# The FFN output product with activations as the stationary operand, and its last three units bank by bank

## The chip, the cores and the metric

The kernel runs on one core of a Trainium2 chip. The metric is the device time of one execution in microseconds (us), as the median of several runs. One execution is also profiled; the profile's times are counted from the first instruction of the program.

## What is computed

Two transformer-like blocks over 256 tokens (T) of width 1024 (D), in float32. The change lies in the end of the second block:

```python
h = modulate(rmsnorm_2(x, norm_ffn_g[l]), sh_f, sc_f)
a, b = jnp.split(h @ w_ffn_in[l], 2, axis=-1)
x = x + g_f[:, None, :] * ((jax.nn.silu(a) * b) @ w_ffn_out[l])
...
return rmsnorm_2(x, norm_final_g)
```

w_ffn_in is 1024 x 5632, w_ffn_out 2816 x 1024. g_f has one value for each of the 1024 features. The final norm divides each token's row by its root mean square over the 1024 features and multiplies by norm_final_g.

## The kernel before

x is kept with features on partitions: 8 chunks of 128 features, each 128 x 256 tokens. Every product is made of three matmuls (`mm3`, lines 156 to 161): each float32 operand is split into a rounded part and the rest (hi and lo), and hi*hi, lo*hi and hi*lo are summed in PSUM. The first operand of a matmul is the stationary one, which is loaded into the array; the second is moved through it.

Weights come in units of 128 x 1024. `unit_order` (line 1453) lists them in the order of use. SyncE loads two units at a time (line 92), ScalarE or VectorE rounds one to hi (lines 106 and 108), VectorE subtracts to get lo (line 116). `fill` (line 97) keeps this some five units ahead of the use, and is called whenever a unit is taken (`w`, line 120).

The order of instructions on each engine is the order of the program text; each engine takes its own instructions strictly in that order. A DMA is issued by the engine on whose queue the text puts it, and its wait stands in that engine's order.

The FFN is the last part of `block2`, from line 1365 on. It first makes the norm's row factor and the modulated input (`h`, lines 1368 and 1369), then the scaled gate `hgf` (line 1371, 128 x 8, feature within its chunk on partitions), then finishes two pairs of w_ffn_in units whose products were made ahead (lines 1381 to 1388). The loop over the 22 pairs (line 1390) makes, for each j, two products of w_ffn_in (16 x 3 matmuls of 256 columns in all, PSUM tiles from `main`), Tanh on ScalarE (line 1400), two VectorE steps (1401, 1407) and the split into fh and fl (1408, 1409): 128 hidden features x 256 tokens. From j = 3 on it takes unit j-3 of w_ffn_out in `kunit` (line 242): for each of the 8 chunks of output features the weights are stationary (128 x 128) and fh or fl is moved (256 columns), and the sums stay in four PSUM banks over all 22 units, two feature chunks to a bank.

After the loop come the last three units (lines 1419 to 1422). Then, for each chunk, VectorE adds the gated product to x (1428), and TensorE transposes the result to token rows (1431, two 128 x 128 transposes a chunk) into four PSUM tiles. ScalarE squares and sums each (1436), VectorE multiplies each by the final gain `fg` (1438, 1442), and after Ln, Exp (lines 257, 258) and a refining step on VectorE (264 to 266) the rows are scaled (1447, 1449) and written out by four DMAs of 256 KB on SyncE's queue (1450).

Of the kernel before, what the change touches and what calls it, by code (L numbers as in the profile page):

```python
# [13 lines left out]
F32 = mybir.dt.float32  # L14
# [5 lines left out]
AF = mybir.ActivationFunctionType  # L20
OP = mybir.AluOpType
AX = mybir.AxisListType
PSUM = bass.MemoryType.PSUM
DRAM = bass.MemoryType.DRAM

T = 256
D = 1024
# [37 lines left out]
class Kx:  # L65
# [1008 lines left out]
    def block2(self):  # L1074
        nc, tc, a = self.nc, self.tc, self.a
        mt = self.mod[1]
        x = self.x
        with ExitStack() as ctx:
            big = ctx.enter_context(tc.tile_pool(name="b2", bufs=1))
            tmp = ctx.enter_context(tc.tile_pool(name="b2t", bufs=2))  # L1080
            self.side_cycle = ("s",)
            fg = self.sm("final_g")
# [75 lines left out]
            z = big.tile([128, 4, PAD + T], F32, name="z")  # L1158
# [57 lines left out]
            for c in range(4):  # L1216
# [7 lines left out]
                else:  # L1224
                    if c == 2:
                        p, pz = self.units("w_u", 4, h, lambda i: self.bank(2 + i), False)
                        self.fill()
                    else:
                        p = self.unit("w_u", 2 * c, h)
# [13 lines left out]
            p = self.unit("w_qi", 4, h)  # L1243
# [5 lines left out]
            for u in range(4):  # L1249
                p = self.unit("w_qi", u, h)  # L1250
# [59 lines left out]
            for u in range(8):  # L1310
                p = self.unit("w_qk", u, h)
# [11 lines left out]
            for u in range(16):  # L1323
                p = self.unit("w_g", u, h)
# [7 lines left out]
            for n in range(8):  # L1332
                if n % 2 == 0:
                    w = self.w("w_conv_proj", n // 2)
                p = self.main()[:, :T]
# [8 lines left out]
            banks = [self.bank(i) for i in range(4)]  # L1344
            for n in range(9):
                if n < 8:
                    if n % 2 == 0:
                        w = self.w("w_attn_proj", n // 2)
                    p = self.main()[:, :T]
                    self.chunk(w, (ah, al), p, nk=4, off=(n % 2) * 512)  # L1350
                    t = gates[:, n]
# [13 lines left out]
        with ExitStack() as ctx:  # L1365
            big = ctx.enter_context(tc.tile_pool(name="f2", bufs=1))
            tmp = ctx.enter_context(tc.tile_pool(name="f2t", bufs=5))
            rstd = self.row_rstd(self.ps_x[:, :T], "exp_and_others")
            h = self.modulated(rstd, gn, mt[:, 24:32])
            hgf = big.tile([128, 8], F32, name="hgf")  # L1370
            nc.scalar.mul(hgf, mt[:, 40:48], 0.5)
            nf = a["w_ffn_out"].shape[0]
            fg = big.tile([128, 2, 512], F32, name="fg")
            act = {}

            def ffn_out(j):
                self.kunit("w_ffn_out", j, act.pop(j), banks, j == 0, j == nf - 1)

            raw = [[tmp.tile([128, T], F32, name=f"st{k}", bufs=2) for k in range(3)] for _ in range(2)]
            bias = []  # L1380
            for j in range(2):
                t, b = self.settle_raw(2 * j, rstd, raw[j][0])
                bias.append((b, self.settle_raw(2 * j + 1, rstd, raw[j][1])[1]))
                self.fill(self.pos + 4 + j, self.pos + 4 + j)
                half = self.normp.tile([128, 1], F32, name="stb", bufs=6)
                nc.vector.tensor_scalar(half, b, 0.5, None, op0=OP.mult)
                nc.scalar.activation(raw[j][2], t, AF.Tanh, bias=half, scale=0.5)
                nc.scalar.activation(t, t, AF.Identity, bias=b)
            self.fill(self.pos + 6, self.pos + 6)
            for j in range(nf):  # L1390
                sa = tmp.tile([128, T], F32, name="sa")
                if j < 2:
                    p, q, th = raw[j]
                else:
                    if j == 2:
                        p, q = self.units("w_ffn_in", 4, h, lambda i: self.side(), False)
                    else:
                        p = self.unit("w_ffn_in", 2 * j, h)
                    th = sa
                    nc.scalar.activation(th, p, AF.Tanh, scale=0.5)  # L1400
                nc.vector.scalar_tensor_tensor(sa, th, 1.0, p, op0=OP.add, op1=OP.mult)
                if j > 2:
                    q = self.unit("w_ffn_in", 2 * j + 1, h)
                if j < 2:
                    nc.vector.scalar_tensor_tensor(sa, q, bias[j][1], sa, op0=OP.add, op1=OP.mult)
                else:
                    nc.vector.tensor_tensor(sa, q, sa, op=OP.mult)
                act[j] = tuple(tmp.tile([128, T], F32R, name=n) for n in ("fh", "fl"))
                self.split(*act[j], sa)
                if j == 3:  # L1410
                    banks = [self.bank(i) for i in range(4)]
                if j == 2:
                    self.fill()
                if j == 10:
                    nc.sync.dma_start(fg, bass.AP(tensor=a["gf"].tensor, offset=a["gf"].offset,
                                                  ap=[[0, 128], [512, 2], [1, 512]]))
                if j >= 3:
                    ffn_out(j - 3)
            for j in range(nf - 3, nf - 1):
                ffn_out(j)  # L1420
            self.lnexp()
            ffn_out(nf - 1)
            tok = [[self.main(), self.main()], [self.side(), self.side()]]
            z = big.tile([128, 2, 2, 512], F32, name="z")
            ss = [big.tile([128, 2], F32, name=f"ss{i}") for i in range(2)]
            for n in range(8):
                xc = x[:, n]
                nc.vector.scalar_tensor_tensor(xc, banks[n // 2][:, (n % 2) * T:(n % 2 + 1) * T], hgf[:, n:n + 1], xc,
                                               op0=OP.mult, op1=OP.add)
                for tt in range(2):  # L1430
                    nc.tensor.transpose(tok[tt][n // 4][:, (n % 4) * 128:(n % 4 + 1) * 128],
                                        xc[:, tt * 128:(tt + 1) * 128], self.ident)
            for i in range(2):
                for tt in range(2):
                    junk = tmp.tile([128, 512], F32, name="junk", bufs=2)
                    nc.scalar.activation(junk, tok[tt][i], AF.Square, scale=1.0 / 32, accum_out=ss[i][:, tt:tt + 1])
            for tt, i in ((0, 0), (1, 0), (0, 1)):
                nc.vector.tensor_tensor(z[:, tt, i], tok[tt][i], fg[:, i], op=OP.mult)
            ms = tmp.tile([128, 2], F32, name="ms")
            nc.vector.tensor_tensor(ms, ss[0], ss[1], op=OP.add)  # L1440
            rs = self.rsqrt_start(ms, [128, 2], tmp)
            nc.vector.tensor_tensor(z[:, 1, 1], tok[1][1], fg[:, 1], op=OP.mult)
            rstd = self.rsqrt_end(rs)
            for tt, i in ((0, 0), (1, 1), (1, 0), (0, 1)):
                y = z[:, tt, i]
                if tt == i == 1:
                    nc.scalar.mul(y, y, rstd[:, tt:tt + 1])
                else:
                    nc.vector.tensor_scalar(y, y, rstd[:, tt:tt + 1], None, op0=OP.mult)
                nc.sync.dma_start(self.out[tt][:, i * 512:(i + 1) * 512], y)  # L1450


def unit_order():
# [145 lines left out]
```

## Time and profile before

| | us |
|---|---|
| median of 3 runs | 1450.75 (1449.32 to 1452.83) |
| the profiled execution | 1445.74 |
| its span, first to last instruction | 1443.7 |
| TensorE busy | 1367.2 (95%) |
| VectorE busy | 1098.1 (76%) |
| ScalarE busy | 770.9 (53%) |
| FFN, from the gate to the end | about 190 |

TensorE's busy time is that of pipelined matmuls: a matmul of 256 columns is shown with 0.28 us, but the next one starts 0.12 us after it. What counts for the pace is the distance between starts. The chain that ended last is put down to TensorE for 71%, to VectorE for 21%, to ScalarE for 3% and to DMA for 3%. In the text PE is TensorE, PEld its loading of stationary operands, DVE is VectorE, ACT ScalarE, SP SyncE.

### The profile page before, as it was taken

To read this page: it belongs to the slowest core of one execution; us is meant where nothing else is said; L and a number is where in the kernel's file an instruction comes from. 1 tells how busy PE (TensorE), PEld (TensorE's weight loads), DVE (VectorE), ACT (ScalarE), POOL (GpSimd) and SP (SyncE) were. 2 spreads that over 40 slices of the span, in tenths; PEclk is the share of its full clock that TensorE was granted. 3 is DMA by queue.
4 is the path that set the end of the run, shared out by engine and by line. 5 is a ranking of instruction groups with operands and counts; after the bars stand their busy time and mean duration, and the time that the engine had idled before them with its cause. 6 is when DMAs were issued, how large, how long until landed. Compare 5 with 4: busy or idle time off the path is not lost.

```text
span 1443.7 us, 27450 instructions
## 1 busy us (share of the span) xinstructions
PE 1367.2 (95%) x11208; PEld 1321.7 (92%) x11208; DVE 1098.1 (76%) x2105; ACT 770.9 (53%) x1247; POOL 115.4 (8%) x93
## 2 busy tenths in 40 slices
PE   3888999989999999999999999999999899999997
PEld 2767889979999999999999999999999889999997
DVE  7887899996999487777777766666799968765554
ACT  3535665444999545454444454444565484644442
POOL 0020010000000000000000000000167620100000
PEclk8999999999999999999999999999999999999999
DMA  9566554544777888888888867766445335345551
GB/s 376 182 210 216 207 178 147 177 145 146 263 275 280 321 307 291 297 305 315 306 295 283 287 228 240 235 218 219 144 163 175 117 109 208 123 175 190 180 196 64
DMA packets 106062, 317.31 MB, mean 220 GB/s; under 512 B 5584, under 2 KB 34640, under 8 KB 103632
## 3 DMA queue, kind: packets, MB, share of 16 engines
q1 hardware_dynamic: 65696, 250.54, 49.5%
q10 hardware_dynamic: 39408, 61.87, 12.2%
q0 software_dynamic: 832, 3.15, 0.7%
q8 instruction: 88, 1.44, 0.4%
q14 instruction: 38, 0.31, 0.1%
HBM read 297.71 MB, written 17.83 MB: 219 GB/s over the span
## 4 chain that ended last, share of the span: by engine, by line
PE 71%; DVE 21%; ACT 3%; DMA 3%; issue 2%; POOL 0%; POOLq 0%; DVEq 0%; SPq 0%; ACTq 0%
PE m L159 12%; PE m L160 12%; PE m L161 12%; PE a L160 11%; PE a L161 10%; PE a L159 10%; DVE wlo L116 5%; DVE a L1168 3%; DVE junk L322 2%; PE s L983 2%; DMA raw<-in_ada_w 1%; DMA mraw<-in_ada_w 1%; DVE score L1127 1%; DVE cacc L552 1%; ACT whi L108 1%
## 5 line engine op out<-in xcount | busy, mean ns | idle before, releaser
L159 PE MATMUL m<-hi,whi 128*128 128x256 f32 x1816 | 519.3, 286 | 7.1 <-DVE cacc L552 4.0
L161 PE MATMUL m<-hi,wlo 128*128 128x256 f32 x1816 | 509.8, 281 | 2.8 <-POOL wlo L116 1.5
L160 PE MATMUL m<-lo,whi 128*128 128x256 f32 x1816 | 509.6, 281 | 0.0
L116 DVE TENSOR_TENSOR wlo<-raw,whi 128x1024 fp32r<-128x1024 f32 x398 | 479.0, 1222 | 36.3 <-ACT whi L108 25.8
L108 ACT CAST whi<-raw 128x1024 fp32r<-128x1024 f32 x428 | 444.4, 1045 | 50.9 <-DMA raw<-in_peer_v 17.9
L159 PEld LDWEIGHTS m<-hi,whi 128*128 128x128 f32 x1816 | 343.7, 189 | 10.0 <-issue 4.2
L161 PEld LDWEIGHTS m<-hi,wlo 128*128 128x128 f32 x1816 | 343.3, 189 | 3.4 <-DVE wlo L116 1.7
L160 PEld LDWEIGHTS m<-lo,whi 128*128 128x128 f32 x1816 | 343.3, 189 | 0.6
L161 PE MATMUL a<-wh,wlo 128*128 128x256 f32 x1024 | 288.3, 282 | 0.0
L160 PE MATMUL a<-wl,whi 128*128 128x256 f32 x1024 | 288.2, 281 | 0.0
L159 PE MATMUL a<-wh,whi 128*128 128x256 f32 x1024 | 287.9, 281 | 0.0
L161 PEld LDWEIGHTS a<-wh,wlo 128*128 128x128 f32 x1024 | 192.9, 188 | 0.0
L160 PEld LDWEIGHTS a<-wl,whi 128*128 128x128 f32 x1024 | 192.7, 188 | 0.0
L159 PEld LDWEIGHTS a<-wh,whi 128*128 128x128 f32 x1024 | 192.6, 188 | 0.0
L1024 DVE TENSOR_TENSOR wl<-act,wh 128x256 fp32r<-128x256 f32 x128 | 54.5, 425 | 140.5 <-PE a L160 125.2
L790 ACT ACTIVATE act<-m 128x256 f32<-128x256 f32 x126 | 48.4, 384 | 167.2 <-PE m L161 167.2
L1019 ACT CAST wh<-act 128x256 fp32r<-128x256 f32 x128 | 51.9, 406 | 145.4 <-DVE act L1012 121.5
L322 DVE SCALAR_TENSOR_TENSOR junk<-mraw,silu 128x1024 bf16<-128x1024 f32 x80 | 97.5, 1219 | 7.5 <-DMA mraw<-in_ada_w 6.9
L116 POOL TENSOR_TENSOR wlo<-raw,whi 128x1024 fp32r<-128x1024 f32 x33 | 79.2, 2425 | 36.0 <-ACT whi L108 26.5
L986 ACT ACTIVATE stg<-s 128x512 f32<-128x512 f32 x64 | 64.2, 1108 | 3.1 <-PE s L983 1.0
L1012 DVE TENSOR_TENSOR act<-act,gt 128x256 f32<-128x256 f32 x128 | 53.6, 419 | 8.2 <-DMA gt<-gd 8.2
L159 PE MATMUL a<-fh,whi 128*128 128x256 f32 x176 | 50.6, 287 | 3.4 <-ACT fh L250 3.4
(443 smaller groups left out, 1772.8 us busy)
## 6 DMA issues: line engine op xcount, KB each, us to landing
raw<-in_peer_u SPq DMA_DIRECT2D x64, 1024.0 KB, 6.0
raw<-in_peer_v SPq DMA_DIRECT2D x64, 1024.0 KB, 5.1
mraw<-in_w_ada ACTq DMA_DIRECT2D x48, 512.0 KB, 5.5
raw<-in_w_ffn_in SPq DMA_DIRECT2D x22, 1024.0 KB, 5.1
gd<-stg ACTq DMA_DIRECT2D x16, 1024.0 KB, 6.2
gt<-gd ACTq DMA_DIRECT2D x14, 1024.0 KB, 7.5
mraw<-in_ada_w SPq DMA_DIRECT2D x24, 512.0 KB, 4.4
raw<-in_w_ffn_out SPq DMA_DIRECT2D x11, 1024.0 KB, 4.9
```

Of the source, the lines that this page charges most:

```text
L108: self.nc.scalar.copy(t, self.raw[k])
L116: eng.tensor_tensor(t, self.raw.pop(k), h.bitcast(F32), op=OP.subtract)
L159: mm(out, w[0], x[0], start=start, stop=False, **kw)
L160: mm(out, w[0], x[1], start=False, stop=False, **kw)
L161: mm(out, w[1], x[0], start=False, stop=stop, **kw)
L322: self.nc.vector.scalar_tensor_tensor(junk, w, 0.5, self.silu_c[i], op0=OP.mult, op1=OP.mult, accum_out=self.mod[i][:, u:u + 1])
L790: nc.scalar.activation(t, p, AF.Gelu)
L986: nc.scalar.mul(stg[:, :, e0:e0 + 4].rearrange("p i t -> p t i"), p, 1.0 / GSCALE)
L1012: nc.vector.tensor_tensor(tv, tv, gv, op=OP.mult)
L1019: nc.scalar.copy(wts[b], acts[b])
L1024: nc.vector.tensor_tensor(wl, acts.pop(b), wts[b].bitcast(F32), op=OP.subtract)
L1168: nc.vector.scalar_tensor_tensor(zp, z[:, c, k:k + T], w, zp, op0=OP.mult, op1=OP.add)
```

## The change

- The product with w_ffn_out is made the other way round: fh and fl, 128 tokens at a time, are stationary, and 512 columns of the weights are moved. A unit is 2 token halves x 2 column halves x 3 matmuls of 512 columns. Each of the four banks now holds one token half and one half of the output features, in token rows.
- The gate must then be a row that is the same on all partitions. It is written to a DRAM tile `grow` with features in order, and read back into all 128 partitions (`gb`), both by DMAs on ScalarE's queue, right after line 1371.
- x is transposed to token rows (`xt`) during the loop, in four groups of four transposes after j = 5, 7, 9 and 11, each group copied out of PSUM by ScalarE.
- The last three units run bank by bank: for each of the four banks the nine matmuls of all three units, and then that bank's gate, residual, square and final gain; after both banks of a token half its norm and output.

```diff
             def ffn_out(j):
-                self.kunit("w_ffn_out", j, act.pop(j), banks, j == 0, j == nf - 1)
+            def ffn_out(j, w, tt, i):
+                s, m = slice(tt * 128, (tt + 1) * 128), slice(i * 512, (i + 1) * 512)
+                self.mm3(banks[2 * tt + i], [t[:, s] for t in act[j]], [t[:, m] for t in w], j == 0, j == nf - 1)
+
+            drp = ctx.enter_context(tc.tile_pool(name="f2d", bufs=1, space=DRAM))
+            grow = drp.tile([8, 128], F32, name="grow")
+            nc.scalar.dma_start(grow.rearrange("c p -> p c"), hgf)
+            gb = big.tile([128, 2, 512], F32, name="gb")
+            nc.scalar.dma_start(gb.rearrange("p i f -> p (i f)"),
+                                grow.rearrange("c p -> (c p)")[None, :].to_broadcast([128, D]))
+            xt = big.tile([128, 2, 2, 512], F32, name="xt")
+
+            def x_rows(g):
+                tt, i = divmod(g, 2)
+                p = self.side()
+                for c in range(4):
+                    nc.tensor.transpose(p[:, c * 128:(c + 1) * 128], x[:, 4 * i + c, tt * 128:(tt + 1) * 128], self.ident)
+                nc.scalar.copy(xt[:, tt, i], p)
...
                 if j >= 3:
-                    ffn_out(j - 3)
-            for j in range(nf - 3, nf - 1):
-                ffn_out(j)
+                    w = self.w("w_ffn_out", j - 3)
+                    for tt in range(2):
+                        for i in range(2):
+                            ffn_out(j - 3, w, tt, i)
+                    act.pop(j - 3)
+                if j in (5, 7, 9, 11):
+                    x_rows((j - 5) // 2)
             self.lnexp()
-            ffn_out(nf - 1)
...
-            for n in range(8):
-                xc = x[:, n]
-                nc.vector.scalar_tensor_tensor(xc, banks[n // 2][:, (n % 2) * T:(n % 2 + 1) * T], hgf[:, n:n + 1], xc,
-                                               op0=OP.mult, op1=OP.add)
-                for tt in range(2):
-                    nc.tensor.transpose(tok[tt][n // 4][:, (n % 4) * 128:(n % 4 + 1) * 128],
-                                        xc[:, tt * 128:(tt + 1) * 128], self.ident)
...
+            ends = range(nf - 3, nf)
+            ws = [self.w("w_ffn_out", j) for j in ends]
             z = big.tile([128, 2, 2, 512], F32, name="z")
+            for tt in range(2):
+                ss = tmp.tile([128, 2], F32, name="ss", bufs=2)
+                for i in range(2):
+                    for j, w in zip(ends, ws):
+                        ffn_out(j, w, tt, i)
+                    y = z[:, tt, i]
+                    nc.vector.tensor_tensor(y, banks[2 * tt + i], gb[:, i], op=OP.mult)
+                    nc.vector.tensor_tensor(y, y, xt[:, tt, i], op=OP.add)
                     junk = tmp.tile([128, 512], F32, name="junk", bufs=2)
+                    nc.scalar.activation(junk, y, AF.Square, scale=1.0 / 32, accum_out=ss[:, i:i + 1])
+                    if i == 0:
+                        nc.vector.tensor_tensor(y, y, fg[:, i], op=OP.mult)
+                ms = tmp.tile([128, 1], F32, name="ms", bufs=2)
+                nc.vector.tensor_tensor(ms, ss[:, 0:1], ss[:, 1:2], op=OP.add)
+                rs = self.rsqrt_start(ms, [128, 1], tmp)
+                nc.vector.tensor_tensor(z[:, tt, 1], z[:, tt, 1], fg[:, 1], op=OP.mult)
+                rstd = self.rsqrt_end(rs)
+                for i in range(2):
+                    y = z[:, tt, i]
+                    if i:
+                        nc.scalar.mul(y, y, rstd)
+                    else:
+                        nc.vector.tensor_scalar(y, y, rstd, None, op0=OP.mult)
+                    nc.sync.dma_start(self.out[tt][:, i * 512:(i + 1) * 512], y)
```

## Rows read from the trace of the kernel before

**Rows 1.** Busy time by stretch: engines with instruction counts, granted clock, DMA share, GB/s.

```profile
1265.00:1270.60 5.60, 4.88 (x24) 4.48 (x24) 3.31 (x9) 2.83 (x7) 0.00 (x0) 0.70 0.01 1
1270.60:1424.30 153.70, 153.68 (x1296) 153.68 (x1297) 87.13 (x112) 67.53 (x93) 0.00 (x0) 1.00 0.52 182
1433.10:1443.70 10.60, 1.76 (x17) 1.52 (x14) 5.43 (x14) 3.64 (x11) 0.00 (x0) 0.83 0.27 99
```

**Rows 2.** The chain that ended last, 1257 to 1271 us: start, us, what.

```profile
1257.13 0.52 ACT st L1387
1258.18 0.95 ACT whi L108
...
1270.62 0.38 PE m L159
```

**Rows 3.** TensorE in order of time: last three w_ffn_out units, first and last of 72.

```profile
1424.31 0.28 PE L159 MATMUL a<-fh,whi 128*128 128x256 f32 x1
...
1432.83 0.28 PE L161 MATMUL a<-fh,wlo 128*128 128x256 f32 x1
```

**Rows 4.** TensorE in order of time: the w_v stage, first and last of 48.

```profile
1106.03 0.40 PE L159 MATMUL a<-whi,hi 128*128 128x512 f32 x1
...
1116.99 0.40 PE L161 MATMUL a<-whi,lo 128*128 128x512 f32 x1
```

**Rows 5.** TensorE in order of time: the transposes of the end, first and last of 16.

```profile
1432.95 0.27 PE L1431 MATMUL m<-ident,x 128*128 128x128 f32 x1
...
1434.59 0.27 PE L1431 MATMUL s<-ident,x 128*128 128x128 f32 x1
```

**Rows 6.** ScalarE in order of time, with the idle time before and its releaser.

```profile
1254.49 0.19 ACT L1371 ACTIVATE hgf<-mod 128x8 f32<-128x8 f32 x1
1257.13 0.51 ACT L1387 ACTIVATE st<-st,stb 128x256 f32<-128x256 f32 x1 [2.44 <-DVE stb L1386]
...
1276.66 1.05 ACT L108 CAST whi<-raw 128x1024 fp32r<-128x1024 f32 x1 [2.01 <-DMA raw<-in_w_ffn_out]
...
1290.81 0.38 ACT L1400 ACTIVATE sa<-m 128x256 f32<-128x256 f32 x1 [2.94 <-PE m L161]
```

**Rows 7.** Line 1002, the gather gt on ScalarE's queue: issue (ns), and issue to landing.

```profile
L1002 ACTq DMA_DIRECT2D gt<-gd x14: 525/526/589, 521.6 to 976.0; - x14
...
DMA to landing us min/median/max: 5.6/8.0/13.3
```

**Rows 8.** Line 1450, the output DMAs: SyncE in order of time; issue (ns), and landing.

```profile
1438.29 1.82 SPq L1450 DMA_DIRECT2D out_y<-z  x4
...
L1450 SPq DMA_DIRECT2D out_y<-z x4: 361/436/449, 1438.3 to 1439.7; - x4
...
DMA to landing us min/median/max: 2.0/2.4/2.7
```

**Rows 9.** ScalarE and VectorE in order of time, the end of the program.

```profile
1433.91 0.60 ACT L1436 ACTIVATE junk<-m 128x512 f32<-128x512 f32 x1 [10.12 <-PE m L1431]
...
1436.62 0.30 ACT L257 ACTIVATE rs_t<-ms,eps 128x2 f32<-128x2 f32 x1 [0.29 <-DVE ms L1440]
1436.95 0.20 ACT L258 ACTIVATE rs_y<-rs_t 128x2 f32<-128x2 f32 x1
1437.77 0.72 ACT L1447 ACTIVATE z<-z,rs_y 128x512 f32<-128x512 f32 x1 [0.62 <-DVE rs_y L266]
...
1434.64 0.69 DVE L1438 TENSOR_TENSOR z<-m,fg 128x512 f32<-128x512 f32 x1 [0.42 <-ACT junk L1436]
...
1436.44 0.15 DVE L1440 TENSOR_TENSOR ms<-ss,ss 128x2 f32<-128x2 f32 x1
...
1437.19 0.16 DVE L264 SCALAR_TENSOR_TENSOR rs_t<-ms,rs_y 128x2 f32<-128x2 f32 x1
1437.38 0.16 DVE L265 SCALAR_TENSOR_TENSOR rs_t<-rs_t,rs_y 128x2 f32<-128x2 f32 x1
...
1437.77 1.28 DVE L1449 TENSOR_SCALAR z<-z,rs_y 128x512 f32<-128x512 f32 x3
```

**Rows 10.** Groups of instructions (page, part 5): count, busy us, mean ns, idle before.

```profile
L116 DVE TENSOR_TENSOR wlo<-raw,whi 128x1024 fp32r<-128x1024 f32 x398 | 479.0, 1222 | 36.3 <-ACT whi L108 25.8
```

**Rows 11.** Busy time by stretch around the gate's scaling, columns as in rows 1.

```profile
1254.00:1256.00 2.00, 2.00 (x17) 1.85 (x16) 1.82 (x8) 0.61 (x2) 0.00 (x0) 1.00 0.00 0
```

More of the change, by code (lines that the diff above doesn't have):

```diff
@@ L1374, in block2 @@
             act = {}
-            def ffn_out(j):
-                self.kunit("w_ffn_out", j, act.pop(j), banks, j == 0, j == nf - 1)
+            def ffn_out(j, w, tt, i):
[14 more added lines that the diff above has]
+                nc.scalar.copy(xt[:, tt, i], p)
             raw = [[tmp.tile([128, T], F32, name=f"st{k}", bufs=2) for k in range(3)] for _ in range(2)]
@@ L1423, in block2 @@
-            tok = [[self.main(), self.main()], [self.side(), self.side()]]
+            ends = range(nf - 3, nf)
+            ws = [self.w("w_ffn_out", j) for j in ends]
             z = big.tile([128, 2, 2, 512], F32, name="z")
-            ss = [big.tile([128, 2], F32, name=f"ss{i}") for i in range(2)]
-            for n in range(8):
-                xc = x[:, n]
-                nc.vector.scalar_tensor_tensor(xc, banks[n // 2][:, (n % 2) * T:(n % 2 + 1) * T], hgf[:, n:n + 1], xc,
-                                               op0=OP.mult, op1=OP.add)
-                for tt in range(2):
-                    nc.tensor.transpose(tok[tt][n // 4][:, (n % 4) * 128:(n % 4 + 1) * 128],
-                                        xc[:, tt * 128:(tt + 1) * 128], self.ident)
@@ L1433, in block2 @@
-            for i in range(2):
-                for tt in range(2):
-                    junk = tmp.tile([128, 512], F32, name="junk", bufs=2)
[L1436 to L1450, printed above, removed]
+            for tt in range(2):
[6 more added lines that the diff above has]
+                    nc.vector.tensor_tensor(y, y, xt[:, tt, i], op=OP.add)
+                    junk = tmp.tile([128, 512], F32, name="junk", bufs=2)
+                    nc.scalar.activation(junk, y, AF.Square, scale=1.0 / 32, accum_out=ss[:, i:i + 1])
[13 more added lines that the diff above has]
+                    nc.sync.dma_start(self.out[tt][:, i * 512:(i + 1) * 512], y)
```

## The prediction, made before the changed kernel was run

> **What bounds the kernel now.** I read the granted clock and busy time by stretch first, then the chain of work that ended last, then the instructions of the last 190 us in order of time. The change touches only the second block's FFN. There the stretches [rows 1] show two regimes. From 1270.6 to 1424.3 us TensorE is busy for all but 0.02 us at the full granted clock, while VectorE is busy for 87 of the 154 us and ScalarE for 68: TensorE's pace alone sets the time. From 1433.1 us to the end TensorE works for 1.8 us of 10.6, and a serial chain of VectorE, ScalarE and output DMAs sets it. Ahead of both lies a third piece: around 1257 us the chain runs through ScalarE (Tanh of line 1387, then a weight cast) and only reaches TensorE at 1270.62 [rows 2]. So an edit is worth something in one of three ways: TensorE columns per second in the loop, the length of the last chain, or a delay of ScalarE before the loop.
>
> **The change part by part.**
>
> **Product with swapped operands.** Before, a unit of w_ffn_out is 24 matmuls of 256 columns; the first of the last 72 starts at 1424.31 and the last at 1432.83 [rows 3], so 8.52/71 = 0.1200 us each and 2.880 us a unit. After, it is 12 matmuls of 512 columns with activations stationary, which is just what the w_v stage runs: 48 matmuls from 1106.03 to 1116.99 [rows 4], 10.96/47 = 0.2332 us each, 2.798 a unit. That saves 0.082 us a unit. Of the 19 units in the loop the first hides: it runs while TensorE is ahead of the others (TensorE busy 4.88 of 5.60 us between 1265.0 and 1270.6, at a mean granted clock of 0.70, between the 1.2 and the 2.4 GHz level [rows 1]) and the chain passes elsewhere [rows 2]. So 18 units count: 18 x 0.082 = -1.5 us up to the start of the last three units. The Trainium skill, "TensorE: Matmul & The Clock Gate", section "Back-to-back issue gap", gives a warm matmul N/2.4 ns plus 2.5 ns, thus about 0.216 us for 512 columns and 0.109 for 256; by that the unit would fall from 2.62 to 2.59 us, an estimate from that page, and 18 units would save 0.6 us. The rows are slower at both widths, and the sum goes by the rows.
>
> **Rows of x.** Sixteen 128x128 transposes move out of the end into the loop (j = 5, 7, 9, 11). Sixteen stand in the trace right behind a matmul of the same kind, from 1432.95 to 1434.59 [rows 5]: 1.64/15 = 0.109 us each, first to last without a gap. In the loop TensorE is the bound, so all 16 x 0.109 = +1.75 us count. The four ScalarE copies out of PSUM (about 0.6 us each, the duration of Square from the same kind of tile [rows 9]) wait for transposes that stand behind a whole unit on TensorE, so ScalarE's next weight cast and Tanh queue behind them. The cover is ScalarE's 2.94 us wait ahead of each Tanh [rows 6], which the copy and the moved cast fit into; without it TensorE would lose 0.6 us four times. I price it at nothing.
>
> **gate as a row.** Between the scaling of the gate (line 1371) and the Tanh of line 1387 ScalarE now issues two DMAs: the 128x8 gate to DRAM as 1024 separate 4-byte elements, and its broadcast back (512 KB), which must wait, on ScalarE's in-order queue, until the first has landed. Behind that wait stand Tanh, Identity and the weight cast of lines 1387, 1388 and 108; VectorE waits for those, and TensorE at 1270.62 for VectorE. The cover is ScalarE's idle time: the gate is done at 1254.68, Tanh starts at 1257.13 [rows 6]. No row shows a DMA of 4-byte elements. Nearest are the output (128 packets of 2 KB, at best 2.0 us from issue to landing [rows 8]) and the gather gt (2048 packets of 512 B, at best 5.6 us, median 8.0 [rows 7]). Between those two best cases the price is (5.6-2.0)/(2048-128) = 1.9 ns per packet, and 1024 packets would land after 2.0 + 896 x 0.0019 = 3.7 us. An element of 4 bytes should cost less than a packet of 512 B, so I take the middle of 2.0 and 3.7, 2.8 us. Then the second issue ends at 1254.72 + 2.8 + 0.03 + 0.45 (an issue takes 0.36 to 0.53 [rows 7, 8]) = 1258.0, and the chain is late by **+0.9 us**; the ends are +0.1 (landing 2.0) and +1.8 (3.7), the far end +6.1 (8.0, gt's median). A gain is excluded, since Tanh's other input is ready only at 1257.1. The broadcast's data runs beside one weight load and costs nothing: the first weight cast after it that waits for a load stands at 1276.66 [rows 6], and TensorE doesn't stop there either [rows 1]. The Trainium skill, "DMA: Bandwidth & Descriptors", section "Rules for kernel authors", says a non-contiguous last dimension becomes one descriptor per element and should be rearranged; its section "Measured" gives 10.5 ns a packet as the floor for small ones. By that, 64 packets on each of 16 engines add 0.7 us to the 2.0, the chain would be late by 0.8, and the sum would hardly move (an estimate from that page).
>
> **The last three units, bank by bank.** Let t = 0 be the start of their first matmul, 1424.31 before. Bank 0 (9 matmuls) is ready at 8 x 0.2332 + 0.40 = 2.27, the banks after that at 4.37, 6.47 and 8.56. On each bank VectorE multiplies by the gate (0.69), adds x (0.69), ScalarE squares, and VectorE multiplies in place by the final gain (0.69), which must wait until Square has read. An elementwise 512-column operation takes 0.69 from PSUM [rows 9]; from SBUF the row is 1.22 for 1024 columns [rows 10], so 0.61 to 0.69, and I take 0.69. Square now reads SBUF: the SBUF row of ScalarE is 0.72 against 0.60 from PSUM, and with the read of the sum 0.10 more, 0.82 [rows 9]. A dependent instruction starts 0.03 after its releaser. For one half of the tokens this is a chain: 5 elementwise operations (3.45, less 0.08 for the one overlap), 2 Squares (1.64), the sum ms (0.15), Ln 0.30, Exp 0.20, three small steps (0.48) and twelve hand-overs (0.36): 6.50 us. It starts at 2.30, the final scaling follows at 8.80, and because VectorE is in order the second half's first multiplication comes only at 9.20, though its bank was ready at 6.47. So the second half's scaling starts at 9.20 + 6.50 = 15.70, where before it started at 1437.77 - 1424.31 = 13.46. TensorE, done at 8.56, isn't the bound any more, and the 0.24 us that the three units save is worth little. At the end there are two output DMAs instead of four: the last issue starts at 15.70 + 0.48 + 0.03 + 0.45 = 16.66; before it was 1439.66 (the last 0.45 of 1438.29 to 1440.11 [rows 8]), and the span ended 4.04 later. With two of 256 KB queued and not four the last lands some 0.5 earlier (2.2 instead of 2.7). End: 16.66 + 3.54 = 20.20 against 1443.7 - 1424.31 = 19.39, **+0.8 us**; with the six SBUF operations of the chain at 0.61 it is +0.3, with 0.05 for each of the 24 hand-overs +1.3.
>
> **Sum:** -1.5 + 1.75 + 0.9 + 0.8 = +2.0 us. The profiled execution (1445.74, span 1443.7) would become 1447.7. The median of the runs shown, 5 us above it, becomes 1450.75 + 2.0 = 1452.7.
>
> **Rivals.** (A) The gate's round trip is dear: 4-byte elements land no faster than gt. From a landing of about 3.7 us on it decides the sign that can be measured. At gt's median of 8.0 the chain is late by 6.1 and the sum is -1.5 + 1.75 + 6.1 + 0.8 = +7.2: 1457.9; at 5.6 it is +4.8, 1455.5. For it: nothing like it is in the trace. Against: the DMA engines carry nothing at that time [rows 11].
> (B) The 512-column form runs at the array's rate here: 512 columns at the 2.4 GHz level are 0.213 us. Then a unit is 2.56, 18 units save 5.8 instead of 1.5, the sum is -2.3 and the time 1448.4. For it: the clock is granted in full here [rows 1]. Against it: 47 steps of the same form at 0.2332 [rows 4]. The Trainium skill's rule for a matmul's gap, cited above, comes to nearly the same pace, 0.216.
> (C) VectorE is free when the last bank is ready (the second half would have to overtake the first half's wait for Exp): scaling then starts at 8.56 + 0.03 + 0.69 + 0.72 + 0.85 + 0.18 + 0.56 + 0.60 = 12.2, 3.5 earlier, the sum is -1.5 and the time 1449.2. In-order issue, seen all through the end [rows 9], speaks against.
>
> **How the numbers follow.** About 0.2%, 2.9 us, is what a measurement of this kernel can tell from no change. The forecast has 0.60: of that 0.52 lies within 2.9 us, 0.05 above (a landing of 3.7 with a slow end), 0.03 below. A has 0.25, all of it slower. B has 0.09, C 0.06; they give -2.3 and -1.5 us, and half of each passes 2.9 by the bounds of the other terms. So faster 0.03 + 0.045 + 0.03, rounded to 0.11; same 0.52 + 0.045 + 0.03, rounded to 0.59; slower 0.05 + 0.25 = 0.30. The range reaches down to B and C with 0.4 for the spread of runs (1449.3 to 1452.8 now), 1448.0, and up to the better part of A, 1457.0.
>
> **What would show it.** Right: 12 matmuls a unit at 0.233 us; four groups of 4 transposes at 0.11; ScalarE idle between the gate and Tanh until about 1258 us, with the wait on the round trip; VectorE the last chain from t = 2.3 on, the second half's first multiplication long after its bank was ready; end 20 us after the last three units began. Wrong: a pace other than 0.233; Tanh still at 1257.1, or past 1259; a VectorE chain that waits for TensorE again at the last bank; TensorE gaps at j = 5 to 12.

## The result: slower by 0.7%, and the profile after

The changed kernel takes 1460.07 us (median; 1455.92 to 1468.58), the kernel before beside it 1451.12: a ratio of 1.0069, 95% interval 1.0051 to 1.0086. That is about 10 us by the ratio and 9 by the two medians. The prediction was 1452.7 us with a range up to 1457.0: wrong in size, and slower beyond doubt where "no change that can be measured" had most of the chance.

The profiled execution has a span of 1458.5 us against 1443.7. Of these 14.8 us, 4.94 lie ahead of the edit: the scaling of the gate (line 1371) starts at 1259.43 instead of 1254.49 [rows 6]. Everything ahead of it is the same code, and in the executions profiled for this study that start lies anywhere from 1254.5 to 1261.8. So I compare from the gate's start on, in two pieces: up to the first matmul of the last three units, and from there to the end of the span.

| us | gate to last three units | last three units to end |
|---|---|---|
| before | 169.82 | 19.39 |
| after | 179.20 | 19.87 |
| after - before | **+9.38** | **+0.48** |

Together +9.86, which fits the measured 9 to 10. The last three units of the changed kernel start here (TensorE in order of time):

```profile
1438.63 0.40 PE L159 MATMUL a<-whi,fh 128*128 128x512 f32 x1
```

Where the 9.38 went stands in the chain of waits of the changed kernel, 1255 to 1280 us (start, us, what):

```profile
1259.43 0.20 ACT hgf L1371
1259.65 11.42 DMA grow<-hgf
1271.09 0.34 ACTq L1384
```

The same in ScalarE's instructions in order of time (the brackets give the idle time before and its releaser). Before, Tanh waited 2.44 us, and for VectorE [rows 6]; now:

```profile
1259.43 0.20 ACT L1371 ACTIVATE hgf<-mod 128x8 f32<-128x8 f32 x1
1259.65 0.40 ACTq L1382 DMA_DIRECT2D grow<-hgf  x1
1271.09 0.34 ACTq L1384 DMA_DIRECT2D gb<-grow  x1
1271.48 0.51 ACT L1403 ACTIVATE st<-st,stb 128x256 f32<-128x256 f32 x1 [11.86 <-DMA grow<-hgf]
```

11.86 less 2.44 is 9.42, the loss of the stage to 0.04 us. TensorE runs out of work meanwhile. The stretches (length, PE, PEld, DVE, ACT, POOL busy, granted clock, DMA share, GB/s), which answer [rows 1]:

```profile
1267.00:1271.90 4.90, 0.00 (x0) 0.00 (x0) 0.00 (x0) 0.41 (x1) 0.00 (x0) 0.71 0.38 79
1272.00:1290.00 18.00, 9.60 (x54) 8.36 (x55) 11.23 (x20) 9.64 (x16) 0.00 (x0) 0.70 0.29 104
1290.00:1436.00 146.00, 146.00 (x1045) 136.64 (x1044) 80.50 (x103) 65.13 (x90) 0.00 (x0) 1.00 0.53 185
```

The clock of 0.70 behind the stall, between the 1.2 and the 2.4 GHz level, is no extra loss: before, it was 0.70 at this place too [rows 1], and the stage lost no more than the wait. From 1290 us on the loop is what it was: no idle time on TensorE, the clock granted in full. The DMA issues of 1255 to 1280 us (KB each, us from issue to landing) show the write at 11.4 us, and a weight load beside it at 14.0; third, the load at the same place in the kernel before, 6.3:

```profile
raw<-in_w_ffn_in SPq DMA_DIRECT2D x1, 1024.0 KB, 14.0
grow<-hgf ACTq DMA_DIRECT2D x1, 4.0 KB, 11.4
...
raw<-in_w_ffn_in SPq DMA_DIRECT2D x1, 1024.0 KB, 6.3
```

And the odd part: between 1260.5 and 1261.3 us the DMA engines show all of the write's small packets (1024 elements and 16 more), and after that none of them, so that the data seem to be under way for 0.8 us of the 11.4:

```profile
DMA packets 1040, 0.00 MB, mean 5 GB/s; under 512 B 1040, under 2 KB 1040, under 8 KB 1040
```

From there until the write has landed the weight load moves at 40 GB/s (columns as above), where the load before ran at 258 from 1258 to 1260 us; it lands 5.0 us after the write:

```profile
1262.60:1271.10 8.50, 3.79 (x34) 3.59 (x32) 0.22 (x1) 0.00 (x0) 0.00 (x0) 0.88 0.28 40
```

### The profile page after: what moved, and what is told of

It is laid out like the page before. It is cut to its first block, busy times and chain, and to the rows that moved or that the text cites. A ratio compares the mean times of both kernels' runs of the same rounds, so it can differ in the third digit from the quotient of the medians.

```text
span 1458.5 us, 26931 instructions
## 1 busy us (share of the span) xinstructions
PE 1369.2 (94%) x10944; PEld 1310.7 (90%) x10944; DVE 1100.8 (75%) x2108; ACT 774.9 (53%) x1254; POOL 116.0 (8%) x93
## 4 chain that ended last, share of the span: by engine, by line
PE 72%; DVE 20%; ACT 4%; DMA 2%; issue 1%; POOL 0%; POOLq 0%; ACTq 0%; SPq 0%; DVEq 0%
PE m L159 12%; PE m L161 12%; PE m L160 12%; PE a L160 11%; PE a L161 10%; PE a L159 10%; DVE wlo L116 4%; DVE a L1168 3%; PE s L983 2%; DVE junk L322 2%; DMA raw<-in_ada_w 1%; DVE score L1127 1%; DMA grow<-hgf 1%; DVE cacc L552 1%; ACT whi L108 1%
## 5 line engine op out<-in xcount | busy, mean ns | idle before, releaser
L216 POOL TENSOR_TENSOR act<-act 128x256 f32<-128x256 f32 x7 | 6.6, 938 | 549.3 <-ACT act L207 548.6
```

## The experiments

Each kernel is given as its difference from the kernel after or the kernel before. "The stage" is gate to last three units of the table above, in the profiled execution; "..." stands for lines left out. The question of the first four was which part of the change costs what.

**The wait moved off ScalarE.** From after, one word:

```diff
-            nc.scalar.dma_start(gb.rearrange("p i f -> p (i f)"),
+            nc.gpsimd.dma_start(gb.rearrange("p i f -> p (i f)"),
```

> The changed kernel with one edit: the broadcast of the gate row back into SBUF, and with it the wait for the write's landing, is issued from GpSimd's queue, on which nothing stands in this stage; the write of 1024 elements stays on ScalarE's queue. Theory W (the whole loss is ScalarE standing in that wait, 9.4 us on the chain): Tanh starts again right after its VectorE input, about 2.4 us after the gate, though the write still lands after about 11 us; the total is before +0.4 us, ratio 1.000 to 1.001. Rival M (the small writes hold up the memory for all, the weight load beside them landed after 14 us instead of 6): Tanh starts on time, but a weight cast waits for its load and TensorE loses several us; ratio 1.003 or more. Rival P (the pace, the transposes and the tail cost more than the trace shows): ratio 1.004 or more with no wait at either place.

Measured: 1449.52 us against 1450.93, ratio 0.9993 [0.9979, 1.0006]. The write lands no sooner (12.9 us), and the load beside it is as late (15.0); but GpSimd has nothing else to do and takes the wait:

```profile
1275.47 0.58 POOL L1384 DMA_DIRECT2D gb<-grow  x1 [25.40 <-DMA grow<-hgf]
```

```profile
1264.42 0.51 ACT L1403 ACTIVATE st<-st,stb 128x256 f32<-128x256 f32 x1 [2.44 <-DVE stb L1402]
```

Tanh's wait is 2.44 us and ends with VectorE, as before the change, and the stage is 169.81 us, as before to 0.01. So the late landing alone costs nothing here, nor does the late weight load: all of the loss is the in-order queue behind the wait. It also shows that the swapped product and the rows of x together come to nothing.

**The gate written as rows.** From after: TensorE transposes the gate to 8x128, ScalarE copies it out, and the write has 8 rows of 512 bytes; the wait stays on ScalarE.

```diff
-            nc.scalar.dma_start(grow.rearrange("c p -> p c"), hgf)
+            pg = self.side()
+            nc.tensor.transpose(pg[:8, :128], hgf, self.ident)
...
+            nc.scalar.copy(hrow, pg[:8, :128])
+            nc.scalar.dma_start(grow, hrow)
```

> The changed kernel, but the gate is first transposed on TensorE to 8 x 128, copied out by ScalarE, and written as 8 rows of 512 bytes; both DMAs and the wait stay on ScalarE's queue. Theory E (it is the separate 4-byte writes that land late): the write lands after 2 to 3 us, Tanh starts some 4 us after the gate instead of 12, the total is before +1 to +2.5 us, ratio about 1.001. Rival R (a round trip through DRAM at this place is slow in any layout): landing 8 to 11 us, ratio 1.006.

Measured: 1450.05 us against 1450.93, ratio 0.9996 [0.9982, 1.0009]; stage 169.81 us. ScalarE in order of time:

```profile
1258.39 0.54 ACTq L1386 DMA_DIRECT2D grow<-hrow  x1
1259.66 0.36 ACTq L1388 DMA_DIRECT2D gb<-grow  x1
1260.19 0.51 ACT L1407 ACTIVATE st<-st,stb 128x256 f32<-128x256 f32 x1 [1.83 <-DVE stb L1406]
```

The same 4 KB has landed when the read back is issued, 1.27 us after the write's issue (2 to 3 were expected), and Tanh starts 2.64 us after the gate, as before. So the form of the write is what is dear, not the trip through memory.

**The round trip alone.** From before: the two DMAs of the gate added where the change has them, their result unused.

```diff
+            nc.scalar.dma_start(grow.rearrange("c p -> p c"), hgf)
...
+            nc.scalar.dma_start(gb.rearrange("p i f -> p (i f)"),
+                                grow.rearrange("c p -> (c p)")[None, :].to_broadcast([128, D]))
```

> The kernel before with the two gate DMAs alone added at the same place on ScalarE's queue; their result is not used. Theory W: before +9 to +10 us, ratio 1.006 to 1.007, Tanh 12 us after the gate. Rival P (the loss sits in the swapped product, the transposes or the tail): before +0 to +1, ratio 1.000.

Measured: 1460.21 us against 1450.93, ratio 1.0062 [1.0039, 1.0085]; landing 12.2 us, stage 180.03 us: +10.21 to the kernel before. ScalarE's wait ahead of Tanh, less the 2.44 of before, is 10.21 as well:

```profile
1271.73 0.51 ACT L1393 ACTIVATE st<-st,stb 128x256 f32<-128x256 f32 x1 [12.65 <-DMA grow<-hgf]
```

These two instructions by themselves cost as much as the whole change.

**The end in another order.** From the first experiment: each half's steps are reordered by hand, and three of the four multiplications by the final gain go to GpSimd. The order is (head: gate, x, Square; gain: final gain; out: scaling and output):

```python
            head(0, 0); gain(nc.gpsimd, 0, 0)
            head(0, 1); gain(nc.gpsimd, 0, 1); rs0 = norm(0)
            head(1, 0); gain(nc.gpsimd, 1, 0)
            r0 = self.rsqrt_end(rs0); out(0, 1, r0)
            head(1, 1); out(0, 0, r0); rs1 = norm(1)
            gain(nc.vector, 1, 1); r1 = self.rsqrt_end(rs1)
            out(1, 0, r1); out(1, 1, r1)
```

> As e1 (the wait on GpSimd's queue), and the end is reordered: VectorE takes the second token half's gate and residual ahead of the first half's refining steps and scaling, and three of the four multiplications by the final gain go to GpSimd. Theory V (after the loop the in-order VectorE chain sets the end, not TensorE): the second half's scaling starts 12.5 us after the last three units begin instead of 15.4, total e1 -2.9 us, ratio to before about 0.998. Rival T (TensorE or ScalarE is the bound there, or GpSimd's multiplications hold VectorE up): as e1, or slower.

Measured: 1449.87 us, ratio 0.9996 [0.9981, 1.0012]. The end takes 18.8 us instead of 19.9 in the kernel after: a gain, but not the 2.9 expected, and the time shows none against the first experiment (1449.52). VectorE and GpSimd in order of time:

```profile
1435.48 0.69 DVE L1453 TENSOR_TENSOR z<-a,gb 128x512 f32<-128x512 f32 x1 [0.68 <-PE a L161]
1436.21 1.28 DVE L1454 TENSOR_TENSOR z<-z,xt 128x512 f32<-128x512 f32 x1
...
1441.26 1.55 DVE L1454 TENSOR_TENSOR z<-z,xt 128x512 f32<-128x512 f32 x1
```

```profile
1435.65 1.29 POOL L1459 TENSOR_TENSOR z<-z,fg 128x512 f32<-128x512 f32 x1 [160.44 <-ACT junk L1456]
...
1441.00 1.26 POOL L1459 TENSOR_TENSOR z<-z,fg 128x512 f32<-128x512 f32 x1 [1.38 <-ACT junk L1456]
```

The additions of x, 0.69 us alone, take 1.28, 1.09 and 1.55, and each ends some 0.55 us after the GpSimd operation beside it (1437.49 after 1436.94, 1442.81 after 1442.26), while the multiplication that reads PSUM keeps its 0.69. The Trainium skill, "SBUF — State Buffer", section "SBUF: two separate sides", says a VectorE operation with two SBUF inputs and a GpSimd operation lock each other out. The rows agree on which operations suffer, and in all three pairs GpSimd had started first. If the addition waited for GpSimd's whole instruction, it should end a whole 0.69 us behind it, not 0.55; what the difference comes from was not tried.

**The same end without GpSimd.** From the kernel of the last experiment: one gain moves into a gap of VectorE, two are merged with the final scaling (stt: one VectorE instruction for gain and scaling, and the output), and ScalarE scales the first quarter. The order is now:

```python
            head(0, 0); head(0, 1); gain(nc.vector, 0, 0); rs0 = norm(0)
            head(1, 0); r0 = self.rsqrt_end(rs0)
            y = z[:, 0, 0]; nc.scalar.mul(y, y, r0); nc.sync.dma_start(self.out[0][:, :512], y)
            head(1, 1); stt(0, 1, r0); rs1 = norm(1)
            gain(nc.vector, 1, 1); r1 = self.rsqrt_end(rs1)
            stt(1, 0, r1); out(1, 1, r1)
```

> As b1, but GpSimd does nothing at the end: one multiplication by the final gain is done by VectorE in a gap, two are merged with the scaling in one VectorE instruction, one stays; ScalarE scales the first quarter. Theory G (in b1 VectorE's additions took 1.28 and 1.09 and 0.85 us longer in their rows because GpSimd's multiplications ran beside them): the additions are back at 0.69 us, the second half's scaling starts 12.5 us after the last three units begin (13.7 in b1, 15.4 in the changed kernel), the end comes after some 17.3 us (18.7 in b1, 19.4 before), ratio to before about 0.9985. Rival (the additions were slow for another reason, such as TensorE's writes to the banks): they stay above 1 us and the end comes after 18.5 us or more.

Measured: 1446.44 us against 1450.41, ratio 0.9970 [0.9958, 0.9982]: faster than both kernels. VectorE in order of time:

```profile
1437.00 0.69 DVE L1454 TENSOR_TENSOR z<-z,xt 128x512 f32<-128x512 f32 x1
1437.61 0.75 DVE L1476 SCALAR_TENSOR_TENSOR z<-z,rs_y,fg 128x512 f32<-128x512 f32 x1
...
1439.82 0.75 DVE L1476 SCALAR_TENSOR_TENSOR z<-z,rs_y,fg 128x512 f32<-128x512 f32 x1
```

Additions are back at 0.69, the merged step costs 0.75 where the two it replaces cost 0.68 and 0.48, and the second half's scaling starts 12.15 us after the last three units began (15.40 in the kernel after). The end takes 17.2 us, 2.2 less than the kernel before, and the stage is 169.81: the change's idea pays once the wait and the order of the end are mended. The trace so accounts for 2.2 of the 4 us between the medians; where the rest comes from is not shown.

**Why the write lands so late.** Half the elements first: this kernel writes and broadcasts only 512 gate values and uses them for both halves of the columns.

```diff
-            nc.scalar.dma_start(grow.rearrange("c p -> p c"), hgf)
+            nc.scalar.dma_start(grow.rearrange("c p -> p c"), hgf[:, :4])
...
```

> The changed kernel with half the gate: only 4 of the 8 columns are written and read back, 512 elements, and serve both halves of the features (this leaves out the other half of the gate values). Theory E (each 4-byte write costs its share of the landing): landing 2 + 9.4/2 = 6.7 us, Tanh 4.7 us earlier than in the changed kernel. Rival F (a fixed price for a DMA with elements, or for write and read back): landing stays at 11 us.

Measured: landing 12.3 us, Tanh idle 12.75, stage 180.08, 1460.84 us against 1453.62. Half the elements are no sooner there, so a price per element, as theory E has it, falls. Two probes followed, from before: five writes each whose result nobody reads, issued by ScalarE inside the loop, that differ in the number and spacing of their 4-byte elements.

```diff
+            probes = {6: (pa.rearrange("c p -> p c"), hgf), 9: (pb[:, :, 0].rearrange("c p -> p c"), hgf),
+                      12: (pc, hgf), 15: (pd.rearrange("c p -> p c"), hgf[:, :4]),
+                      18: (pe.rearrange("c p -> p c"), hgf[:, :2])}
...
+                if j in probes:
+                    nc.scalar.dma_start(*probes[j])
```

and, in the second,

```diff
+            probes = {6: (pa.rearrange("c p -> p c"), hgf[:, :1]), 9: (pb[:, :, 0].rearrange("c p -> p c"), hgf),
+                      12: (pc[:, :, 0].rearrange("c p -> p c"), hgf), 15: (pd[:, :, 0], hgf),
+                      18: (pe[:, :, 0].rearrange("c p -> p c"), hgf[:, :2])}
```

> The kernel before with five extra writes of the gate to DRAM on ScalarE's queue, far apart in the FFN loop, that nobody waits for: 1024 elements next to each other (after j = 6), 1024 elements 256 bytes apart (9), 128 rows of 32 bytes (12), 512 elements (15), 256 elements (18). Theory E (a price per 4-byte write): landings of about 11, 11, 3, 6.5 and 4.3 us. Rival L (it is writes to the same stretch of memory that wait for each other): the elements 256 bytes apart land in 3 us. Rival F (a fixed price): 11 us for all with elements. The weight loads beside the slow ones take longer under the first two; the total time stays at that of before within 3 us.

> The kernel before with five extra writes of the gate to DRAM that nobody waits for, on ScalarE's queue in the FFN loop: 128 elements next to each other (after j = 6), 1024 elements 32 bytes apart (9), 1024 elements 64 bytes apart (12), 1024 elements 8 bytes apart with the 8 of a partition together (15), 256 elements 256 bytes apart (18). Theory L (writes to the same short stretch of memory wait for each other, some 0.6 us for each; 16 of them make the 11 us): landings of about 9, 6, 6, 6 and 3 to 6 us. Theory E (a price per element, some 0.01 us): 3, 11, 11, 11 and 4 us. Rival F (any DMA of elements that are neighbours in memory is slow as a whole): 9 for the first and 3 to 6 for the others.

The first probe's DMA issues (KB, us to landing): pb is 1024 elements 256 bytes apart, pc 128 rows of 32 bytes, pd 512 and pe 256 packed elements (pa, 1024 packed, has no landing in the records).

```profile
pb<-hgf ACTq DMA_DIRECT2D x1, 4.0 KB, 6.0
pc<-hgf ACTq DMA_DIRECT2D x1, 4.0 KB, 3.7
pd<-hgf ACTq DMA_DIRECT2D x1, 2.0 KB, 11.9
pe<-hgf ACTq DMA_DIRECT2D x1, 1.0 KB, 9.0
```

The second's: pa is 128 packed elements, pb 1024 at 32 bytes, pc 1024 at 64, pd 1024 at 8 (a partition's eight side by side), pe 256 at 256 bytes.

```profile
pa<-hgf ACTq DMA_DIRECT2D x1, 0.5 KB, 10.2
pb<-hgf ACTq DMA_DIRECT2D x1, 4.0 KB, 5.9
pc<-hgf ACTq DMA_DIRECT2D x1, 4.0 KB, 4.8
pd<-hgf ACTq DMA_DIRECT2D x1, 4.0 KB, 9.1
pe<-hgf ACTq DMA_DIRECT2D x1, 1.0 KB, 3.7
```

128 packed elements land nearly as late as 1024 in the changed kernel (10.2 against 11.4), and 1024 spread ones, eight times as many, in about half of that (4.8 to 6.0, beside weight loads). So spacing weighs far more than number. That is the order of the theory called L, but not its sizes: it had 3 us for the first probe's spread elements (6.0) and 6 for those 8 bytes apart (9.1). Neither kernel moved its time beyond the spread (1448.62 and 1451.97 us).

Another cause would be the weight load that stands beside each of these writes. The second probe's pa rules it out: it was issued at 1300.71 and landed at 1310.94, and in between the DMA engines are idle for 3.4 us (last two columns: DMA share, GB/s) with pa still outstanding:

```profile
1304.50:1307.90 3.40, 3.40 (x31) 3.40 (x30) 1.56 (x2) 1.32 (x2) 0.00 (x0) 1.00 0.00 0
```

The last two kernels put L to the test at the place itself, from before:

```diff
...
+            grow = drp.tile([8, 128, 64], F32, name="grow")
+            nc.scalar.dma_start(grow[:, :, 0].rearrange("c p -> p c"), hgf)
+            gb = big.tile([8, 128], F32, name="gb")
+            nc.scalar.dma_start(gb, grow[:, :, 0])
```

> The kernel before with the gate's write of 1024 elements of 4 bytes at the place where the changed kernel has it, but each element 256 bytes from the next, and a dependent read back of the 1024 elements (unused) issued by ScalarE behind it. Theory L (elements that share a short stretch of memory wait for each other): the write lands as the spread probes did, 4.8 to 6.0 us less some 2 us for the quieter moment, so 3 to 6 us, Tanh starts 3.5 to 6.5 us after the gate in place of 12, the chain is late by 1 to 4 us and the time is 1.0007 to 1.0028 of the kernel before. Theory P (the place: a write whose dependent read stands in the same queue lands late whatever its layout): 11 to 13 us again, Tanh 12 us after the gate, 1.006.

and, in place of that,

```diff
...
+            grow = drp.tile([1, 128], F32, name="grow")
+            nc.scalar.dma_start(grow.rearrange("c p -> p c"), hgf[:, :1])
+            gb = big.tile([128, 128], F32, name="gb")
+            nc.scalar.dma_start(gb, grow.to_broadcast([128, 128]))
```

> The kernel before with one column of the gate, 128 elements of 4 bytes packed into 512 bytes, written at that place, and its broadcast (64 KB, unused) issued by ScalarE behind it. Theory L: the number of elements doesn't matter as long as they are packed, landing 9 to 12 us, Tanh 10 to 12 us after the gate, about 1.005 of the kernel before. A price per element (theory E, fallen at 512 elements): 1 to 3 us, Tanh within 1 us of the kernel before, no difference in time.

ScalarE in order of time, first the spread elements, then the packed column:

```profile
1258.46 0.40 ACTq L1377 DMA_DIRECT2D grow<-hgf  x1
1260.90 1.27 ACTq L1379 DMA_DIRECT2D gb<-grow  x1
1262.22 0.51 ACT L1392 ACTIVATE st<-st,stb 128x256 f32<-128x256 f32 x1 [3.78 <-DVE st L235]
```

```profile
1255.56 0.34 ACTq L1377 DMA_DIRECT2D grow<-hgf  x1
1264.59 0.33 ACTq L1379 DMA_DIRECT2D gb<-grow  x1
1264.97 0.51 ACT L1392 ACTIVATE st<-st,stb 128x256 f32<-128x256 f32 x1 [9.44 <-DMA grow<-hgf]
```

1024 elements that lie 256 bytes apart land 2.4 us after the issue; 128 that lie side by side land after 9.0. (In the first case the releaser named, VectorE, had long been done; Tanh stands behind the second issue, which takes 1.27 us for its 1024 elements.) The weight load issued next took 7.1 us behind the spread write, 12.4 behind the column, and 14.0 to 15.0 behind the packed writes of 4 KB. The spread kernel ran 1450.25 us against 1451.56, ratio 0.9990 [0.9978, 1.0002], with its stage at 171.53, +1.7. The median doesn't show these 1.7 us, and the interval even leaves them out (1.0012); where they are made up is not shown. The column ran 1453.56 once, its stage 176.80: +6.98, and 9.44 - 2.44 is 7.00. L's landing for the spread case was set too late (3 to 6 us), and the slower time it forecast was not seen; its order is borne out, and the theory that the place or the dependent read is the cause falls.

What the runs show is that 4-byte writes that lie side by side land late, long after their packets have left the records, and that the same writes with gaps don't. That they hold each other up within a short stretch of memory is our reading of it; no run shows how. The Trainium skill, "DMA: Bandwidth & Descriptors", section "Specifications", says that a DMA does read-modify-write below 512 bytes. That would fit writes that must follow each other within a stretch, but no run here shows the reads; and size alone doesn't decide, since the spread elements are 4 bytes too and landed in 2.4 us. How long the stretch is stays open: 32 bytes apart was already as good as 256 (5.9 and 6.0), 8 bytes apart was not (9.1), with another order of the elements.

## Why the prediction was wrong, step by step

| term (us) | predicted | measured |
|---|---|---|
| swapped product | -1.5 | -1.5 |
| rows of x | +1.75 | +1.5 |
| gate's round trip | +0.9 (+0.1 to +6.1) | **+9.4** |
| end | +0.8 | +0.5 |
| sum | +2.0 | +9.9 |

**The gate's round trip is the step that failed**, and in it one factor: the landing. Its working is right. With 11.42 in place of 2.8 it gives 1254.72 + 11.42 + 0.48 = 1266.6, or +9.5, and measured is +9.4. The queue, who waits behind it, the 2.44 us of cover [rows 6] and the broadcast that costs nothing were all as written. The landing was taken from packets of 512 bytes and 2 KB, scaled by their number, with the sentence that "an element of 4 bytes should cost less than a packet of 512 B". No row bore that out. For elements that lie apart the number came out near (2.4 measured, 2.8 taken, for as many), though no row of such a write stood behind it; what it left out is where they land. The far end, the gather's 8.0 us median [rows 7], was 3.4 us too near. "The DMA engines carry nothing at that time" [rows 11] held for the two microseconds read there (from 1258 us the next load ran), and was no argument: packed elements are late on idle engines too, as pa shows.

The rule "rearrange", cited there from the Trainium skill, pointed the right way: rows of 512 bytes make the loss vanish. The packet floor cited beside it, which that page gives for loads issued from GpSimd, comes near the 0.8 us in which the packets moved, and says nothing of the landing.

**Rival A** is what happened, with a larger price. Its mechanism, place and sign held; its two prices (5.6 and 8.0 us) both lay below the measured 11.42, so the time fell outside the range. It had 0.25.

**Swapped product.** TensorE in order of time: first and last of the twelve matmuls of a unit; the first of the next unit; the four transposes behind that one; second and last of the 48 matmuls of 256 columns that follow; and the first of three more units:

```profile
1290.71 0.40 PE L159 MATMUL a<-whi,fh 128*128 128x512 f32 x1
...
1293.27 0.40 PE L161 MATMUL a<-whi,fl 128*128 128x512 f32 x1
...
1299.16 0.39 PE L159 MATMUL a<-whi,fh 128*128 128x512 f32 x1
...
1301.95 0.60 PE L1392 MATMUL s<-ident,x 128*128 128x128 f32 x4
...
1302.50 0.28 PE L160 MATMUL m<-lo,whi 128*128 128x256 f32 x1
...
1307.72 0.28 PE L161 MATMUL m<-hi,wlo 128*128 128x256 f32 x1
1307.83 0.39 PE L159 MATMUL a<-whi,fh 128*128 128x512 f32 x1
...
1316.29 0.39 PE L159 MATMUL a<-whi,fh 128*128 128x512 f32 x1
...
1325.17 0.39 PE L159 MATMUL a<-whi,fh 128*128 128x512 f32 x1
```

2.56/11 is 0.2327 us a matmul, as the w_v stage had it (0.2332 [rows 4]), and 2.79 a unit against 2.88. Two units that follow each other without transposes start 8.45 us apart (1290.71 and 1299.16), where 8.53 was the pitch before; over the whole loop the difference is 0.085 for each of 18 units, -1.5, as predicted. Rival B, the array's rate, is out; the rule of the Trainium skill cited with it (0.216), which that page gives for an isolated matmul, is not the pace of this stream either.

**Rows of x.** With a group of transposes in between, the next unit starts 8.67 us later for the first group (1299.16 and 1307.83), 8.88 for the second (1316.29 and 1325.17), and 8.89 and 8.87 for the last two, in place of 8.45. That is 0.22 + 0.43 + 0.44 + 0.42 = +1.5, and with the -1.5 it gives the stage of the first experiment, equal to that before. Three groups cost the 0.109 us a transpose that was predicted. The first is cheaper because 46 steps of the 48 matmuls behind it take 5.22 us, 0.1135 each, in place of 0.118 elsewhere; why is not shown. The copies and the moved casts of ScalarE cost nothing, as priced (TensorE is busy for 146.00 of 146.00 us).

**The end.** VectorE and ScalarE in order of time, from the first bank on (t = 0 is 1438.63):

```profile
1440.93 0.69 DVE L1451 TENSOR_TENSOR z<-a,gb 128x512 f32<-128x512 f32 x1 [2.43 <-PE a L161]
...
1447.69 0.68 DVE L1451 TENSOR_TENSOR z<-a,gb 128x512 f32<-128x512 f32 x1
...
1454.03 0.48 DVE L1467 TENSOR_SCALAR z<-z,rs_y 128x512 f32<-128x512 f32 x1
```

```profile
1442.38 0.63 ACT L1454 ACTIVATE junk<-z 128x512 f32<-128x512 f32 x1 [4.17 <-DVE z L1452]
```

The chain starts at t = 2.30, as predicted; the second half's first multiplication comes at 9.06 (9.20 predicted) without any wait, VectorE being the bound; its scaling starts at 15.40 (15.70 predicted). Here [rows 9] misled by a little: Square reading SBUF takes 0.63, not 0.72, four times over in this chain. The outputs land 2.0 to 2.4 us after their issue, and the end is 19.87 where 20.20 was predicted. Rival C needed VectorE free at the last bank; it never was. But the run whose end was reordered without GpSimd shows what a better order is worth: an end of 17.2 us.

## What to carry to other kernels

A tiny write to memory that steps element by element through a packed row must be priced by where its elements land, not by its bytes or packets; turn it on an engine first, so that it goes out as whole rows, or lay it out with gaps. Whatever its price, put an instruction that waits for a DMA on a queue with nothing behind it: here one word (GpSimd for ScalarE) took all of the 10 us away. And where the trace has no row like an operation, the far end of its cost is not the dearest row at hand, and an argument that it "should cost less" than a neighbour needs a row of its own.

## What the runs showed of the hardware that was not expected

- Packed 4-byte writes to memory land 9.0 to 12.9 us after their issue, whether 128 or 1024 of them, though the packets of 1024 run within 0.8 us; the same 1024 spread 256 bytes apart land in 2.4 us (6.0 beside weight loads), and as 8 rows of 512 bytes in under 1.3.
- The 1 MB weight load issued next behind 512 or 1024 such writes takes 14.0 to 15.0 us in place of 6.3, behind 128 of them 12.4, and behind the spread ones 7.1. In the changed kernel it moves at 40 GB/s until the write has landed.
- GpSimd multiplying from SBUF makes VectorE's additions of two SBUF inputs take 1.09 to 1.55 us instead of 0.69; those with one input in PSUM keep 0.69.
- Behind the first of four groups of four transposes the 48 matmuls of 256 columns went at 0.1135 us each, and at 0.118 behind the other three and elsewhere. Why was not tried.
